# Four 32-column groups of TensorE for the sample group's attention and scans of a hybrid decoder step

## The chip, the cores and the metric

One Trainium2 chip, one of its cores. The time is that of one launch on the device in microseconds, and the median of several runs counts. TensorE (PE) multiplies matrices into PSUM, VectorE (DVE), ScalarE (ACT) and GpSimd (POOL) work on vectors, and the queues of SyncE (SP) and of POOL issue most DMAs. All values are float32. `F32R` (fp32r) is the type that a matmul takes in one pass; plain `F32` operands go in full precision. Where the kernel wants more precision than F32R has, it splits an operand into a rounded part "hi" and a remainder "lo" and adds the products.

## The reference

One layer of a decoder for two groups of tokens with the same weights: a prompt (256 tokens) and a sample group (8 batches of 4 tokens, 32 in all). Each token has 2048 channels. For both groups:

```python
xn = rmsnorm(x);  z, xbc, dt, q, k, v, r, g, gate_a, gate_b = split(xn @ w_in)
a = ssd_scan(silu(conv(xbc)), dt, state_ssd) ; a = rmsnorm(a * silu(z)) @ w_ssd_out      # 32 heads in 4 groups
b = gla_scan(q, k, v, log_sigmoid(g @ w_gla_gate), state_gla) ; b = ... * silu(r) @ w_gla_out  # 4 heads
h = x + (sigmoid(gate_a) * a + sigmoid(gate_b) * b) @ w_mix_out
h = h + softmax(q K^T) V @ w_co        # q = rmsnorm(h) @ w_cq; 4 heads of 512, 256 memory rows per batch
h = h + (silu(gt) * up) @ w_down       # causal ConvFFN of width 5632
y = rmsnorm(h)
```

Every batch of the sample group has its own recurrent states (SSD: 32 x 64 x 128, GLA: 4 x 256 x 512) and its own memory keys and values (256 x 4 x 512 each). The prompt starts from zero states, and its memory keys and values come from `mem_prompt @ w_ck` and `@ w_cv`, which are outputs too. The new states are outputs as well.

## The kernel before

Activations lie transposed: 128 channels on the partitions, the 288 tokens (256 of the prompt, 32 of the sample group) along the free dimension. A projection (`proj_w`, line 112) keeps 128 weight columns in the array and streams the 288 tokens. Weights come as `raw` tiles of up to 512 KB through a ring of three (SP's queue); `wsplit` (lines 92 to 98) makes hi on ScalarE and lo on VectorE; per 128 x 128 block there are three matmuls, hi by hi (line 127), hi by lo (128) and lo by hi (131). One `yield` of it, a step, is 12 matmuls. The first stage (memory keys and values, `mem_proj`, lines 306 to 310) streams 512 weight columns instead. `run(proj_w(dt_load, 48, ...))` between its parts makes dt (32 columns) and the input of the GLA gate (16 columns).

The scans and the attention are generators. `weave(main, bg, n_main, n_bg)` interleaves the steps of a projection (main) with those of a scan (bg), so that the next unit's projection covers the present unit's scan. There are eight units, SSD groups 0 to 3 and GLA heads 0 to 3, with the planned numbers of steps in `N_MAIN` and `N_BG`. After that the program is ordered by Tile's scheduler, by program order and readiness, with an order for each engine that is fixed at build time.

The parts that matter here, all for the 32 sample tokens. They differ by batch, so each batch needs its own right-hand operand, and its 4 tokens are put into a block of 64 weight columns that is zero elsewhere (`diag2`, line 170: 32 columns hi, 32 columns lo):

- SSD (`ssd_scan`, line 620): the state of each batch is transposed (line 777) and split; `inter` (760 to 763) multiplies the 64 columns with its hi and its lo, 512 wide, all adding into one PSUM tile of 64 rows. Line 753 is the product within a batch, head by head. Lines 722 to 724 are the prompt's own heads, in pairs that write to rows 0 to 63 and 64 to 127. Line 812 folds hi and lo rows together by a matmul with `fold` (64 rows).
- GLA (`gla_scan`, line 921): each batch and key half is split and multiplied likewise (`inter`, 1024 and 1025; line 1027 adds the product within the batch); line 1040 makes the state update, line 1053 folds. Lines 951 and 954 make the masks' products, line 874 the gate, with 16 rows. State tiles come from a ring of four, `c4`, that input states (`sin`), output states (`so`) and others share.
- Attention: for each head, `sample_scores` (line 1238) transposes the 8 batches' keys (line 1213), splits them and adds the scores (1254, 1255), 256 wide; `attend` folds them (1268), makes the softmax, transposes it (1287), splits the values and multiplies (1311, 1312), 512 wide, and folds four times (1329). `sample_scores` isn't woven with anything; `attend` is woven with the query projection of the next head, and that of the last head with nothing.
- `h` (the residual stream) sits in SBUF in the one buffer `bigf` from line 1141 on, loaded from a copy of x in DRAM by four DMAs.

Of the kernel before, what the change touches and what calls it, by code (L numbers as in the profile page):

```python
# [36 lines left out]
N_BG = [48] * 4 + [52] * 4  # L37
# [3 lines left out]
def hybrid_step(ctx: ExitStack, tc: tile.TileContext, I: dict, O: list):  # L41
# [32 lines left out]
    fold = const.tile([2 * NS, NS], F32, name="fold")  # L74
    V.tensor_tensor(fold, ident[0:2 * NS, 0:NS], ident[0:2 * NS, NS:2 * NS], ALU.add)
# [36 lines left out]
    def proj_w(load, ncol, X, nk, cons, N=T):  # L112
# [3 lines left out]
        for k0 in range(0, nk, 4):  # L116
            kn = min(4, nk - k0)
            raw = load(k0, kn)
            for s0 in range(0, kn, 2):
# [14 lines left out]
                if k0 + s0 == 2:  # L134
                    flush()
# [34 lines left out]
    def diag2(blk, src):  # L170

        f = blk.rearrange("p b t -> p (b t)")
        w = 2 * NS + NL
        hi = bass.AP(f.tensor, f.offset, [list(f.ap[0]), [w, NB], [1, NL]])
        lo = bass.AP(f.tensor, f.offset + NS, [list(f.ap[0]), [w, NB], [1, NL]])
        split(hi, lo, src.rearrange("p (b l) -> p b l", l=NL))
# [21 lines left out]
    def rstd_from(pl, ssq, n, four=False):  # L198
# [11 lines left out]
    smask = p1.tile([NS, NS], F32, name="smask")  # L210
    G.affine_select(smask, causal[0:NS, 0:NS], pattern=[[-4, NB], [0, NL]], compare_op=ALU.is_ge, fill=0.0, base=0,
                    channel_multiplier=1)
    smaski = p1.tile([NS, NS], I32, name="smaski")
    V.tensor_copy(smaski, smask)
# [5 lines left out]
    rm_s = p1.tile([P, T], F32, name="rm_s")  # L220
    rm_g = p1.tile([P, T], F32, name="rm_g")
    for rm, c in ((rm_s, 128), (rm_g, 64)):
# [3 lines left out]
    acumT = p1.tile([32, T], F32, name="acumT")  # L226
    lrT = p1.tile([48, T], F32, name="lrT")
    tokc = p1.tile([P, 3, 64], F32, name="tokc")
    wtok = p1.tile([P, 4, 32], F32, name="wtok")
    eas = p1.tile([2 * NS, 32], F32, name="eas")  # L230
# [3 lines left out]
    cblk = p1.tile([P, NB, 2 * NS], F32R, name="cblk")  # L234
    att = p1.tile([P, 2, P], F32, name="att")
    ats = p1.tile([NS, NS], F32, name="ats")
    qblk = p1.tile([P, 2, NB, 2 * NS], F32R, name="qblk")
    G.memset(cblk.bitcast(F32), 0.0)
    G.memset(att, 0.0)
    G.memset(ats, 0.0)  # L240
    G.memset(qblk.bitcast(F32), 0.0)
# [3 lines left out]
    x_d = dram.tile([P, KT, T], F32, name="x_d")  # L245

    X = halves(bigr, "xn")
    with pool("p0") as p0:
# [5 lines left out]
        bsel_rep = bsel_rep.rearrange("p r t -> p (r t)")  # L254
        gm_f = p0.tile([P, P], F32, name="gm_f")
# [61 lines left out]
        def prep_mem(kk):  # L317
# [5 lines left out]
            if kk % 2:  # L323
                sq = p0.tile([P, D], F32, name="junk")
                i, q = kk // 2 % 2, kk // 4
                S.activation(sq[:, 0:512], mt[:, i, q * 512:(q + 1) * 512], ACT.Square, accum_out=mss[:, i, q:q + 1])
# [36 lines left out]
        def x_norm():  # L363
            ss = p0.tile([P, 3], F32, name="ss")
# [32 lines left out]
        def x_prep():  # L397
# [23 lines left out]
            V.tensor_copy(bmask, a[:, 0:NB])  # L421

        weave(mem_proj(I["w_cv"], 0, o_pmv), x_norm(), KT, 12)
# [4 lines left out]
        dte = p0.tile([32, T], F32, name="dte")  # L428
        dtT = p0.tile([32, T], F32, name="dtT")
        acol = p0.tile([32, 1], F32, name="acol")  # L430

        def dt_load(k0, kn):
            raw = wp.tile([P, kn, 48], F32, tag="raw", bufs=RB, name="raw")
            for o, c0, n in ((0, O_DT, 32), (32, O_G, 16)):
                nc.sync.dma_start(out=raw[:, :, o:o + n],
                                  in_=I["w_in"][k0 * P:(k0 + kn) * P, c0:c0 + n].rearrange("(k p) n -> p k n", p=P))
            return raw

        def dt_cons(j, a):
            S.activation(dtx, a[0:32], ACT.Identity, bias=dtb)  # L440
            S.copy(lrT[32:48, :], a[32:48])

        run(proj_w(dt_load, 48, X, KT, dt_cons))

        def dt_prep():
# [7 lines left out]
            V.tensor_tensor_scan(acumT, rm_s[0:32, :], dte, 0.0, ALU.mult, ALU.add)  # L453
# [31 lines left out]
            V.tensor_copy(tokc.rearrange("p c x -> p (c x)"), a[:, 0:192])  # L485
            yield
# [8 lines left out]
            S.activation(eas, tokc[0:2 * NS, 2, 32:64], ACT.Exp)  # L495
# [18 lines left out]
    def b2(name):  # L514
        return pa.tile([P, 512], F32, tag="b2", bufs=9, name=name)

    def r2(name):
        return pa.tile([P, 512], F32R, tag="r2", bufs=6, name=name)

    def c4(shape, name):  # L520
        return pa.tile(shape, F32, tag="c4", bufs=4, name=name)
# [7 lines left out]
    def conv_cache(n, ch0, cache):  # L529

        a = mm_tile()
        TR(a[0:27 * n, 0:P], cache.rearrange("p c t -> p (c t)"), ident)
        st = b2("cst")[0:27 * n, 0:P]
        S.copy(st, a[0:27 * n, 0:P])
        nc.sync.dma_start(out=o_pconv[0, :, ch0:ch0 + n * P].rearrange("k (t p) -> k t p", p=P), in_=st[0:3 * n])
        nc.sync.dma_start(out=o_sconv.rearrange("b k c -> (b k) c")[:, ch0:ch0 + n * P].rearrange("k (t p) -> k t p", p=P),
                          in_=st[3 * n:27 * n])
# [49 lines left out]
    def ssd_proj(g, out):  # L587
        xsT = a4("xsT")
        cache = pa.tile([P, 27, 4], F32, tag="cache", bufs=2, name="cache")
        for j2 in range(2):  # L590
            def cons(j, a, j2=j2):
                t = j2 * 2 + j
                conv_silu(4 * g + t, a, xsT[:, t, :], cache[:, :, t])
            yield from proj(I["w_in"], O_XBC + 512 * g + 256 * j2, 256, X, KT, cons)
        late.append(lambda cache=cache: conv_cache(4, 512 * g, cache))
        if g % 2 == 0:
            bcp = [e2("bc") for _ in range(2)]
            for w in range(2):
# [949 lines left out]
```

## Time and profile before

| | us |
|---|---|
| runs, median (lowest to highest of 3) | 2676.44 (2671.35 to 2677.17) |
| the profiled execution, its own time | 2672.26 |
| its span, first to last instruction | 2670.5 |
| TensorE busy | 2648.0 (99%) |
| VectorE busy | 1824.6 (68%) |
| ScalarE busy | 1467.0 (55%) |
| GpSimd busy | 276.0 (10%) |
| DMA | 509.11 MB, mean 191 GB/s |

The stages by the profile: memory keys and values to 208 us (last record of line 310), the eight units' scans to 1237 us (line 833), the second gate to 1375 us (line 1135), the mixing projection to 1488 us (line 1168), the attention with its first query projection to 1716 us (line 1329), the rest of the output projection and the ConvFFN to the end. The page lists engine shares, the chain of waits that ended last (from the last instruction back to whatever released each step), groups of instructions and DMA issues. The timeline lists instructions in order of time: start, length, engine, line, operation, result<-operands, partitions x elements, count. A matmul's length includes its way through the array, and neighbours overlap; so the distance between two starts tells what a matmul costs the engine. A plain F32 matmul shows as two records.

### The profile page before, as it was taken

The numbers are of one execution on the slowest core, as the hardware profiler recorded it, in microseconds if no ns is written. First come the engines' busy times: TensorE is split into PE (matmuls) and PEld (weight loads), VectorE is DVE, ScalarE is ACT, GpSimd is POOL, SyncE is SP. The second block draws the span as 40 slices with busy tenths as digits, with TensorE's granted clock in tenths as the row PEclk, the third lists the DMA queues.
The fourth block names the chain that finished last, engine by engine and source line by source line (L and its number), as shares of the span: only waits on it lengthen the run. The fifth ranks groups of instructions, "written<-read, shape, count | busy, mean of one in ns | idle before, by whom it ended". The sixth has DMA issues, their size and how long they took to land.

```text
span 2670.5 us, 50978 instructions
## 1 busy us (share of the span) xinstructions
PE 2648.0 (99%) x19191; PEld 2537.7 (95%) x19191; DVE 1824.6 (68%) x3809; ACT 1467.0 (55%) x2958; POOL 276.0 (10%) x360
## 2 busy tenths in 40 slices
PE   9999999999999999999999999999999999999998
PEld 7889999999999999999999999899999999999998
DVE  5656777786676667666656676666777677676765
ACT  7656566564646564645445565555545455454545
POOL 2001101000000000000010122202202021110200
PEclk9999999999999999999999999999999999999999
DMA  8676666655575757677665677555555555555553
GB/s 257 204 223 190 177 189 190 188 175 176 169 249 183 230 174 236 196 238 221 185 224 176 205 232 250 185 167 161 171 170 167 167 160 175 169 166 167 164 171 130
DMA packets 433170, 509.11 MB, mean 191 GB/s; under 512 B 22504, under 2 KB 383896, under 8 KB 432604
## 3 DMA queue, kind: packets, MB, share of 16 engines
q1 hardware_dynamic: 408684, 423.16, 51.4%
q0 software_dynamic: 24208, 82.70, 9.5%
q8 instruction: 150, 2.46, 0.4%
q14 instruction: 96, 0.79, 0.1%
q10 hardware_dynamic: 32, 0.01, 0.0%
HBM read 462.65 MB, written 43.12 MB: 189 GB/s over the span
## 4 chain that ended last, share of the span: by engine, by line
PE 96%; DMA 1%; DVE 1%; ACT 1%; issue 0%; SPq 0%; DVEq 0%; ACTq 0%; POOLq 0%
PE acc L127 26%; PE acc L128 26%; PE acc L131 26%; PE acc L306 2%; PE acc L310 2%; PE acc L307 2%; PE acc L1213 1%; PE la L1255 1%; PE mm L1213 1%; PE la L1254 1%; PE mm L1040 1%; PE la L1024 1%; PE la L1025 1%; PE mm L777 1%; DMA raw<-in_w_mix_out_dram 1%; PE mm L998 1%
## 5 line engine op out<-in xcount | busy, mean ns | idle before, releaser
L95 ACT CAST whi<-raw 128x512 fp32r<-128x512 f32 (+1 forms) x1464 | 897.0, 618 | 1011.3 <-PE acc L128 821.1
L97 DVE TENSOR_TENSOR wlo<-raw,whi 128x512 fp32r<-128x512 f32 (+1 forms) x1464 | 987.3, 686 | 677.7 <-ACT whi L95 656.6
L127 PE MATMUL acc<-xn,whi 128*128 128x288 f32 (+1 forms) x1936 | 550.1, 299 | 0.0
L128 PE MATMUL acc<-xn,whi 128*128 128x288 f32 (+1 forms) x1936 | 541.2, 295 | 0.0
L131 PE MATMUL acc<-xn,wlo 128*128 128x288 f32 (+1 forms) x1936 | 411.7, 294 | 0.0
L127 PE MATMUL acc<-hf,whi 128*128 128x288 f32 x1408 | 396.2, 296 | 0.0
L128 PE MATMUL acc<-hf,whi 128*128 128x288 f32 x1408 | 393.6, 295 | 0.0
L127 PEld LDWEIGHTS acc<-xn,whi 128*128 128x128 f32 (+1 forms) x1936 | 362.7, 187 | 13.3 <-issue 4.6
L128 PEld LDWEIGHTS acc<-xn,whi 128*128 128x128 f32 (+1 forms) x1936 | 363.1, 188 | 6.6 <-issue 2.6
L131 PEld LDWEIGHTS acc<-xn,wlo 128*128 128x128 f32 (+1 forms) x1936 | 309.8, 187 | 0.5 <-DVE wlo L97 0.2
L131 PE MATMUL acc<-hf,wlo 128*128 128x288 f32 x1408 | 302.2, 296 | 0.0
L128 PEld LDWEIGHTS acc<-hf,whi 128*128 128x128 f32 x1408 | 265.2, 188 | 0.1
L127 PEld LDWEIGHTS acc<-hf,whi 128*128 128x128 f32 x1408 | 264.7, 188 | 0.1
L131 PEld LDWEIGHTS acc<-hf,wlo 128*128 128x128 f32 x1408 | 225.4, 188 | 0.0
L128 PE MATMUL acc<-pr,whi 128*128 128x288 f32 x704 | 196.5, 295 | 0.0
L127 PE MATMUL acc<-pr,whi 128*128 128x288 f32 x704 | 195.7, 294 | 0.0
L127 PE MATMUL acc<-un,whi 128*128 128x288 f32 x512 | 151.8, 312 | 1.2 <-ACT ma L849 1.0
L131 PE MATMUL acc<-pr,wlo 128*128 128x288 f32 x704 | 147.7, 290 | 0.0
L128 PE MATMUL acc<-un,whi 128*128 128x288 f32 x512 | 143.7, 295 | 0.0
L1380 POOL COPY fsp<-fst 128x16 f32<-128x16 f32 x88 | 104.7, 1214 | 337.1 <-ACT fcg L1386 96.5
L128 PEld LDWEIGHTS acc<-pr,whi 128*128 128x128 f32 x704 | 132.3, 188 | 0.0
L127 PEld LDWEIGHTS acc<-pr,whi 128*128 128x128 f32 x704 | 132.1, 188 | 0.0
(521 smaller groups left out, 4676.3 us busy)
## 6 DMA issues: line engine op xcount, KB each, us to landing
raw<-in_w_in_dram SPq DMA_DIRECT2D x240, 512.0 KB
raw<-in_w_up_dram SPq DMA_DIRECT2D x176, 512.0 KB
raw<-in_w_down_dram SPq DMA_DIRECT2D x88, 512.0 KB
raw<-in_w_ck_dram SPq DMA_DIRECT2D x32, 512.0 KB
raw<-in_w_cv_dram SPq DMA_DIRECT2D x32, 512.0 KB
raw<-in_w_ssd_out_dram SPq DMA_DIRECT2D x32, 512.0 KB
sin<-in_state_gla_dram POOLq DMA_DIRECT2D x32, 512.0 KB, 4.8
out_dram<-so SPq DMA_DIRECT2D x32, 512.0 KB
```

The costliest lines, as they stand in the source:

```text
L95: S.copy(hi, raw)
L97: V.tensor_tensor(lo, raw, hi, ALU.subtract)
L127: MM(a, hi[:, k, cs], xh, start=(k0 + s0 + k == 0), stop=False)
L128: MM(a, hi[:, k, cs], xl, start=False, stop=False)
L131: MM(a, lo[:, k, cs], xh, start=False, stop=(k0 + s0 + k == nk - 1))
L306: MM(accs[m], mn_hi[:, kk, ms_], hi[:, 0, :], start=(kk == 0), stop=False)
L307: MM(accs[m], mn_lo[:, kk, ms_], hi[:, 0, :], start=False, stop=False)
L310: MM(accs[m], mn_hi[:, kk, ms_], lo[:, 0, :], start=False, stop=(kk == KT - 1))
L777: TR(a[:, t * P:(t + 1) * P], sin[:, e, t * P:(t + 1) * P], ident)
L998: MM(a, kt[:, i, k * P:(k + 1) * P], vt[i], start=True, stop=True)
L1213: TR(a[:, d * 256 + m * P:d * 256 + (m + 1) * P], kv[:, m, dd * P:(dd + 1) * P], ident)
L1380: G.tensor_copy(sp[:, :, 0:2], st.rearrange("p (b k) -> p b k", k=2))
```

## The change

For the sample tokens the split operands go. Each batch takes one plain F32 matmul whose 32 weight columns go to one of four groups of 32 output rows, `32 j` to `32 j + 31`; batch `4 q + j` takes group j, and the four groups are added up at the end by one matmul with `fold4` (128 rows). The matmuls of several batches stand together in one run: SSD 8 and two for the product within the batch, GLA 8 twice, scores 16 twice, values 16 once, per group or head. The states are updated in place (`so` goes, `c4` has 6 buffers). Products with fewer than 128 rows or columns are widened to 128 by copies or by zeros (masks, gate, softmax transposes, folds). The prompt's SSD heads go four at a time. `h` is written to DRAM during the mixing projection and read back before the output projection, since the first four batches' values take its buffer; x comes in 8 smaller loads. The last head is woven with the first steps of the output projection. The diff, cut to its core:

```diff
-N_BG = [48] * 4 + [52] * 4
+N_BG = [48] * 4 + [38] * 4
...
-                if k0 + s0 == 2:
+                if k0 + s0 == min(4, nk - 2):
                     flush()
...
+    def diag(blk, src):
+        f = blk.rearrange("p b t -> p (b t)")
+        V.tensor_copy(bass.AP(f.tensor, f.offset, [list(f.ap[0]), [NS + NL, NB], [1, NL]]),
+                      src.rearrange("p (b l) -> p b l", l=NL))
...
             for i in (2, 0, 1):
-                junk = p0.tile([P, D], F32, name="junk")
-                S.activation(junk, xts[i], ACT.Square, accum_out=ss[:, i:i + 1])
-                yield
-                yield
+                for q in range(4):
+                    junk = p0.tile([P, 512], F32, name="junk")
+                    S.activation(junk, xts[i][:, q * 512:(q + 1) * 512], ACT.Square, accum_out=sp4[:, i, q:q + 1])
+                    yield
...
         def dt_load(k0, kn):
-            raw = wp.tile([P, kn, 48], F32, tag="raw", bufs=RB, name="raw")
+            raw = wp.tile([P, kn, 112], F32, tag="raw", bufs=RB, name="raw")
...
+            for k in range(kn):
+                G.tensor_copy(raw[:, k, 48:112].rearrange("p (r n) -> p r n", n=16),
+                              raw[:, k, 32:48].unsqueeze(1).to_broadcast([P, 4, 16]))
             return raw
...
-        run(proj_w(dt_load, 48, X, KT, dt_cons))
+        run(proj_w(dt_load, 112, X, KT, dt_cons))
...
+        mab = pa.tile([P, 2, NS], F32, tag="mab", bufs=1, name="mab")
+        for r in range(4):
+            G.dma_start(out=mab[r * NS:(r + 1) * NS], in_=acum_d[h0:h0 + 8, SEQ:T].rearrange("(a r) t -> r a t", r=4)[r].partition_broadcast(NS))
...
-            MM(a[0:n, t0:t0 + n], bT[:, t0:t0 + n], cT[:, t0:t0 + n], start=True, stop=True)
+            MM(a[:, t0:t0 + n], bT[:, t0:t0 + n] if i < 2 else bsr[:, 0, :], cT[:, t0:t0 + n], start=True, stop=True)
...
+                for w in range(2):
+                    o = w * SEQ
+                    for s in range(3):
+                        for e in range(2):
...
+                            if s == 0:
+                                MM(a[rows, o:o + P], xdt[0][:, hs], pm[:, q, 0:P], start=True, stop=True)
+                            elif s == 1:
+                                MM(a[rows, o + P:o + SEQ], xdt[1][:, hs], pm[:, q, P:SEQ], start=True, stop=False)
+                            else:
+                                MM(a[rows, o + P:o + SEQ], st0[:, hs], pea[:, q, :], start=False, stop=True)
...
         def inter():
-            b, sh, sl = pend.pop(0)
-            MM(ysi[0:2 * NS, :], cblk[:, b, :], sh, start=(b == 0), stop=False)
-            MM(ysi[0:2 * NS, :], cblk[:, b, :], sl, start=False, stop=(b == NB - 1))
+            ysi.append(la_tile())
+            ysa.append(mm_tile())
+            for q in (1, 0):
+                for j in (3, 2, 1, 0):
+                    MM(ysi[0][NS * j:NS * j + NS, :], cdm[:, 4 * q + j, :], sts[4 * q + j], start=(q == 1), stop=(q == 0))
+            for r in range(2):
+                MM(ysa[0][NS * r:NS * r + NS, 256 * r:256 * r + 256], mss[:, r, :], xds[:, 256 * r:256 * r + 256],
+                   start=True, stop=True)
...
             for t2 in range(2):
+                if q == 3 and t2 == 1:
+                    inter()
+                    yield
...
-                MM(a[:, 0:T], gw[:, k * P:(k + 1) * P], lrT[32:48, :], start=True, stop=True)
+                MM(a[:, 0:T], gw3[:, k * P:(k + 1) * P], lr3, start=True, stop=True)
...
-                MM(a[0:64, 288 + 64 * i:352 + 64 * i], kd[:, k, P * i:P * i + 64], qe[:, k, P * i + 64:P * i + P],
+                MM(a[:, 288 + 64 * i:352 + 64 * i], kd[:, k, P * i:P * i + P], qe[:, k, P * i + 64:P * i + P],
...
+        MM(osa, atsl, vst, start=True, stop=False)
+        for q in range(2):
+            for k in (1, 0):
+                for j in (3, 2, 1, 0):
+                    b = 4 * q + j
+                    MM(osa[NS * j:NS * j + NS, :], qdm[:, k, b, :], sins[b][:, k, :], start=False, stop=(q == 1 and k == 0))
+            yield
+            for b in range(4 * q, 4 * q + 4):
...
+                for k in range(2):
+                    a = mm_tile()
+                    MM(a, kb[:, k * P:(k + 1) * P], vst, start=True, stop=True)
+                    V.scalar_tensor_tensor(sin[:, k, :], sin[:, k, :], eb[:, k, SEQ + 4 * b + 3:SEQ + 4 * b + 4], a,
+                                           ALU.mult, ALU.add)
+                    yield
+                nc.sync.dma_start(out=o_sgla[b, h].rearrange("(k p) v -> p k v", p=P), in_=sin)
+                if b + 4 < NB:
+                    load_state(b + 4)
...
+        run(proj(I["w_mix_out"], 256 * j2, 256, mx, KT, cons))
+        G.dma_start(out=h_d[:, 2 * j2:2 * j2 + 2, :], in_=hx[j2])
+        if j2 + 3 < KT // 2:
+            load_x(j2 + 3)
...
+        vq = big.tile([P, 4, 2, 512], F32, tag="bigf", bufs=1, name="vq")
...
+        def scores(q):
+            for d in range(4):
+                for j in (3, 2, 1, 0):
+                    b = 4 * q + j
+                    MM(ssc[NS * j:NS * j + NS, 0:256], xq[:, d, b, :], kT[b][:, d, :], start=(q == 0 and d == 0),
+                       stop=(q == 1 and d == 3))
...
+        for q in (1, 0):
+            for m in range(2):
+                for j in (3, 2, 1, 0):
+                    MM(osa[NS * j:NS * j + NS, :], pms[:, m, 4 * q + j, :], vcs[4 * q + j][:, m, :],
+                       start=(q == 1 and m == 0), stop=(q == 0 and m == 1))
...
+        a = mm_tile()
+        for d in range(4):
+            MM(a[:, d * NS:(d + 1) * NS], os_[:, d * P:(d + 1) * P], fold4, start=True, stop=True)
...
     for hd in range(4):
-        ssc = la_tile()
-        sample_scores(hd, ssc)
-        kp, vp = mem_rows(o_pmk[0, :, hd, :], "kp"), mem_rows(o_pmv[0, :, hd, :], "vp")
-        if hd < 3:
-            weave(q_proj(hd + 1), attend(hd, ssc, kp, vp), 16, 20)
-        else:
-            run(attend(hd, ssc, kp, vp))
+        main = q_proj(hd + 1) if hd < 3 else chain(steps(wo[0], 6), steps(wo[1], 6))
+        weave(main, attend(hd), 16 if hd < 3 else 12, 21)
...
+    for j2 in range(KT // 2):
+        G.dma_start(out=h[:, 2 * j2:2 * j2 + 2, :], in_=h_d[:, 2 * j2:2 * j2 + 2, :])
```

More of the change, by code (lines that the diff above doesn't have):

```diff
@@ L976, in gla_scan @@
         stack_r(vst, a)
-        vts = b2("vts")
-        S.copy(vts[0:NS], a[0:NS, :])
         yield
@@ L1014, in gla_scan @@
         nc.sync.dma_start(out=o_pgla[0, h].rearrange("(k p) v -> p k v", p=P), in_=sprev)
-        load_state(0)
-        load_state(1)
+        for b in range(4):
+            load_state(b)
         yield
         osa = la_tile()
-        pend = []
-        def inter():
-            b, k, sh, sl = pend.pop(0)
-            MM(osa[0:2 * NS, :], qblk[:, k, b, :], sh, start=(b == 0 and k == 0), stop=False)
-            MM(osa[0:2 * NS, :], qblk[:, k, b, :], sl, start=False, stop=(b == NB - 1 and k == 1))
-            if b == 0 and k == 0:
-                MM(osa[0:NS, :], ats, vts[0:NS, :], start=False, stop=False)
@@ L1048, in gla_scan @@
         os_ = b2("os")
[L1049 removed]
+        S.copy(os_, osa)
         yield
@@ L1259, in attend, with rows @@
-    def attend(hd, ssc, kp, vp):
-        ss2 = px.tile([2 * NS, 256], F32, tag="ss2", bufs=1, name="ss2")
-        S.copy(ss2, ssc[0:2 * NS, 0:256])
+    def attend(hd):
+        xq = xqm[hd % 2]
+        loads = [(I["cache_mem_k"][b, :, hd, :], "kc") for b in range(NB)]
+        loads += [(o_pmk[0, :, hd, :], "kp"), (o_pmv[0, :, hd, :], "vp")]
+        loads += [(I["cache_mem_v"][b, :, hd, :], "vc") for b in range(4, NB)]
+        got = []
+        vq = big.tile([P, 4, 2, 512], F32, tag="bigf", bufs=1, name="vq")
+        def rows():
+            while loads and len(got) < 4:
+                got.append(mem_rows(*loads.pop(0)))
+            return got.pop(0)
+        ssc = la_tile()
+        kT = []
+        def scores(q):
[4 more added lines that the diff above has]
+                       stop=(q == 1 and d == 3))
+        for b in range(NB):
+            kc = rows()
+            kT.append(k4("kT"))
+            for d2 in range(2):
+                a = transpose_half(kc, d2)
+                (S.copy if d2 else V.tensor_copy)(kT[b][:, 2 * d2:2 * d2 + 2, :], a)
+            if b < 4:
+                G.dma_start(out=vq[:, b], in_=I["cache_mem_v"][b, :, hd, :].rearrange("(m p) d -> p m d", p=P))
+            yield
+            if b == 4:
+                scores(0)
+                yield
+        kp = rows()
@@ L1266, in attend @@
         yield
[L1267 to L1270 removed]
+        scores(1)
         yield
@@ L1284, in attend @@
             yield
+        vp = rows()
+        vh, vl = v2("vph"), v2("vpl")
+        split(vh, vl, vp)
         a = mm_tile()
         for m in range(2):
-            TR(a[:, m * NS:(m + 1) * NS], pr[:, m * P:(m + 1) * P], ident[0:NS, 0:NS])
+            TR(a[:, m * P:(m + 1) * P], pr[:, m * P:(m + 1) * P], ident)
         for m in range(2):
-            diag2(ptb[:, m], a[:, m * NS:(m + 1) * NS])
-        vcs = [mem_rows(I["cache_mem_v"][b, :, hd, :], "vc") for b in range(2)]
+            f, g = pms[:, m].rearrange("p b t -> p (b t)"), a[:, m * P:(m + 1) * P]
+            V.tensor_copy(bass.AP(f.tensor, f.offset, [list(f.ap[0]), [4 * (NS + NL), 2], [NS + NL, 4], [1, NL]]),
+                          bass.AP(g.tensor, g.offset, [list(g.ap[0]), [4 * NL, 2], [NS + NL, 4], [1, NL]]))
         yield
@@ L1358, in hybrid_step @@
     hf = halves(bigr, "hf")
-    run(residual(I["w_co"], co, vec("norm_ffn"), hf))
+    h = bigf("h")
+    for j2 in range(KT // 2):
+        G.dma_start(out=h[:, 2 * j2:2 * j2 + 2, :], in_=h_d[:, 2 * j2:2 * j2 + 2, :])
+    acc = pb.tile([P, T], F32, tag="sqa", bufs=1, name="sqa")
+    res.update(h=h, hf=hf, acc=acc)
+    run(*wo)
+    rst.append(acc)
     rf = []
```

388 lines of the change are left out of this document (182 added, 206 removed).

## The prediction

> **What bounds the kernel now.** I read the page first: engine shares, then the chain of waits.
>
> ```profile
> PE 2648.0 (99%) x19191; PEld 2537.7 (95%) x19191; DVE 1824.6 (68%) x3809; ACT 1467.0 (55%) x2958; POOL 276.0 (10%) x360
> ...
> PE 96%; DMA 1%; DVE 1%; ACT 1%; issue 0%; SPq 0%; DVEq 0%; ACTq 0%; POOLq 0%
> ```
>
> TensorE is busy throughout and is 96% of the chain that ended last. So the time changes by the TensorE time that the edit takes out, less what it puts in, less new stalls; the ScalarE and VectorE splits that disappear are off the path. A matmul's mean length in a group is no price, since neighbours overlap. I price by the distance between starts in the timeline of TensorE (first number: start in us, second: length). Four prices follow.
>
> Plain fp32, 512 columns (L998), between projection matmuls:
>
> ```profile
> 728.21 1.02 PE L998 MATMUL mm<-vt,kt 128*128 128x512 f32 x2
> 728.66 0.69 PE L127 MATMUL acc<-xn,whi 128*128 128x288 f32 x1
> 729.20 0.29 PE L128 MATMUL acc<-xn,whi 128*128 128x288 f32 x1
> ```
>
> One matmul leaves two records. A projection matmul takes 0.13 (rows below), so L127 really began at 729.20 - 0.13 = 729.07, and L998 took 0.86: 0.43 a record of 512 columns, in proportion for fewer.
>
> The split form (hi and lo in fp32r), which the sample stages use now:
>
> ```profile
> 746.56 0.40 PE L1024 MATMUL la<-sh,qblk 128*64 128x512 f32 x1
> 746.79 0.40 PE L1025 MATMUL la<-sl,qblk 128*64 128x512 f32 x1
> 747.03 0.37 PE L127 MATMUL acc<-un,whi 128*128 128x288 f32 x1
> ```
>
> 0.235 each. For the scores, one batch of the key loop:
>
> ```profile
> 1510.69 0.60 PE L1213 MATMUL mm<-ident,kc 128*128 128x128 f32 x4
> 1511.13 0.60 PE L1213 MATMUL acc<-ident,kc 128*128 128x128 f32 x4
> ...
> 1512.49 0.27 PE L1213 MATMUL mm<-ident,kc 128*128 128x128 f32 x1
> ```
>
> A transpose is 0.11 (0.44 for four; the price of any record with 128 weight columns and few moving ones). The batch takes 1.80; less 8 transposes, 0.92 is left for 8 score matmuls of 256 columns: 0.115 each.
>
> The gap around a narrow run, that is, one using fewer than 128 rows, or fp32 with fewer than 128 output columns:
>
> ```profile
> 750.03 0.43 PE L131 MATMUL acc<-un,wlo 128*128 128x288 f32 x2
> 750.40 1.04 PE L1027 MATMUL la<-vts,ats 32*32 32x512 f32 x2
> ...
> 751.61 0.29 PE L128 MATMUL acc<-un,whi 128*128 128x288 f32 x1
> ```
>
> L131 is done at 750.03 + 0.26 = 750.29, projection is back at 751.61 - 0.13 = 751.48: 1.19 for two records of 0.43. The gap is 0.33 a run, however long the run.
>
> Last, whether groups of columns work at the same time. Before has this in L722 to L724 (two 64-column halves):
>
> ```profile
> 301.92 0.43 PE L131 MATMUL acc<-xn,wlo 128*128 128x288 f32 x2
> 302.28 0.43 PE L722 MATMUL mm<-m,xdt 128*64 128x128 f32 x2
> 302.55 0.27 PE L723 MATMUL mm<-m,xdt 128*64 128x128 f32 x1
> 302.56 0.32 PE L722 MATMUL mm<-m,xdt 128*64 128x128 f32 x1
> 302.66 0.27 PE L723 MATMUL mm<-m,xdt 128*64 128x128 f32 x1
> ...
> 303.59 0.30 PE L128 MATMUL acc<-xn,whi 128*128 128x288 f32 x1
> ```
>
> The second half's L722 (302.56) runs beside the first half's L723 (302.55, 302.66, full pace of 0.11), and starts ahead of its second record. 12 records take 303.46 - 302.18 = 1.28 with the gap; one after another they would be 1.3 without it. Two groups are shown at full speed, four are not.
>
> **The change, stage by stage.** Each batch now takes one plain fp32 matmul with 32 output columns instead of two split ones; four batches fill the four column groups. If all four work together, a round of four costs one matmul: 0.86 at 512 columns, 0.43 at 256.
>
> Attention, per head. Scores: 8 x 4 x 2 x 0.115 = 7.4, now 8 rounds x 0.43 = 3.4 in two runs (0.66). Values: 8 x 2 x 2 x 0.235 = 7.5, now 4 x 0.86 = 3.4 in one run (0.33). The fold of the scores (L1268: 0.43 and a gap) goes; the 32-row transposes (L1287) become two full ones (+0.1, a gap less); four folds of the output (L1329) become one:
>
> ```profile
> 1554.32 0.28 PE L1328 MATMUL mm<-pTh,vpl 128*128 128x256 f32 x1
> 1554.53 0.41 PE L1329 MATMUL mm<-fold,os 64*128 64x32 f32 x2
> ...
> 1555.10 0.30 PE L128 MATMUL acc<-hn,whi 128*128 128x288 f32 x1
> ```
>
> Each is 554.97 - 554.44 = 0.53 (last digits), four 2.1; the new one, 128 rows, no gap, 8 records: 0.9. Per head 3.3 + 3.7 + 0.76 + 0.2 + 1.2 = 9.2; four heads **37**.
>
> GLA, per head:
>
> ```profile
> 1065.85 1.16 PE mm L874 x4
> ...
> 1103.44 1.13 PE mm L951 x12
> 1104.57 0.61 PE mm L954 x8
> ```
>
> (chain of waits: start, time on the chain.) State products: 32 x 0.235 = 7.5, now 3.4 in two runs (0.66): 3.4. The gate (L874), 1.16 + 0.2 of its gap, becomes two fp32r matmuls, 0.26: 1.1. L1027's 1.19 becomes one of 0.235: 0.95. The fold loses its gap: 0.33. L951 and L954, 1.74 and the rest of a gap, about 1.9, widen to 20 records of 0.11 = 2.2: -0.3. Sum 5.5, four heads **22**.
>
> SSD, per group. State products: 16 x 0.235 = 3.8, now 2 x 0.86 + 0.33 = 2.05: 1.7. The intra product (L753, 16 records of 64 columns, 0.9, and a gap) becomes two concurrent matmuls in the same run, 0.43: 0.8. L722 to L724: four runs of 1.28 become two of 12 x 0.11 + 0.33 = 1.65: 1.8. L645 and L812 lose a gap each, about 0.5 together. Sum 4.8, four groups **19**.
>
> Sum: 78 us less TensorE work.
>
> The Trainium skill, "TensorE: Matmul & The Clock Gate", section "Measured speedup vs the span model", gives 2.38x for three column tiles of 512. That is 79% of ideal; as an estimate from that page, the 48 us of grouped rounds here would become about 61 and the saving 13 us less. The rows above show no such loss for two groups.
>
> What is put in. *Projection of dt.* 64 copied columns make each of its loads wait for four POOL copies, with the wsplits and matmuls of L127 queued behind them and the weight ring (three buffers) held.
>
> ```profile
> L1380 POOL COPY fsp<-fst 128x16 f32<-128x16 f32 x88 | 104.7, 1214 | 337.1 <-ACT fcg L1386 96.5 <-DVE fst L1372 69.1 <-ACT fca L1386 56.1
> L547 POOL COPY sp<-scst 128x24 f32<-128x24 f32 x24 | 11.7, 503 | 53.6 <-DVE bc L555 31.7 <-DVE xsT L555 20.1 <-ACT whi L95 1.8
> ...
> 104.91 3.35 SPq L435 DMA_DIRECT2D raw<-in_w_in_dram  x4
> ...
> 117.77 0.43 PE L131 MATMUL acc<-xn,wlo 128*48 128x288 f32 x2
> ```
>
> The last loads are issued at 107 to 108, the stage ends at 118. At 0.5 us a copy a load needs 2 us, hidden by that distance; at 1.2 the 16 copies need 19 from about 102, and the stage ends some 6 late. I take 2.
>
> *The runs' operands.* A run cannot begin until four batches' data are there; what waits behind it on TensorE is the projection. The tightest is GLA's second run: loads of batches 6 and 7 need buffers whose stores have landed.
>
> ```profile
> sin<-in_state_gla_dram POOLq DMA_DIRECT2D x32, 512.0 KB, 4.8
> ```
>
> A load takes 4.8, a store taken as the same: 9.6 from the end of batch 1 to the data of batch 7. Between lie 4 steps of the scan, each with 64/38 = 1.7 projection steps (12 matmuls of 0.13, 1.6) and one 0.235: 4 x 2.9 = 11.7. Just covered. If not, the run is cut up: single groups at 0.86 instead of a round, 8 x 0.86 - 1.7 and three more gaps = 6.2 a head. Between 0 and 25 for four heads; I take 5.
>
> *h in DRAM.* x in 8 loads instead of 4, 8 stores, 8 loads back, all issued by POOL (10% busy). Behind the reload, which waits for the last value run, stand FFN loads that are not due for tens of us. Bandwidth: attention saves 9 of 58 us a head for the same bytes.
>
> ```profile
> 1379.00:1395.00 16.00, 14.08 (x107) 13.84 (x106) 4.41 (x8) 3.36 (x7) 5.38 (x7) 1.00 1.04 399
> 1556.00:1614.00 58.00, 58.00 (x427) 53.21 (x426) 41.21 (x75) 34.54 (x66) 12.79 (x18) 1.00 0.72 238
> ```
>
> 238 GB/s become 238 x 58/49 = 282, under the 399 seen at 1379 (last column): nothing. The last head beside w_co is nearly nothing either: its idle time is small, and the new fold at its end has nothing left beside it (+2).
>
> *Stalls that may go.*
>
> ```profile
> 35.64 0.58 PE L306 MATMUL acc<-whi,mn_hi 128*128 128x512 f32 x1 [3.00 <-ACT whi L95]
> ...
> 1379.77 14.18 DMA raw<-in_w_mix_out_dram
> ...
> 1707.30 0.45 PE L1311 MATMUL la<-vh,ptb 128*64 128x512 f32 x1 [0.69 <-ACT vh L167]
> ```
>
> The first is ScalarE in long squares of x, which are cut in four; the second a weight load beside the burst that loads h, which is spread out; the third a value split. Together 0 to 6, I take 4.
>
> Net: 78 - 2 - 5 - 2 + 4 = 73. The profiled execution took 2672.3 (span 2670.5): 2599. The median of the runs, 2676.4, lies 4.2 higher: **2603**.
>
> **Rivals.**
>
> *Two at a time* (0.08). Each matmul is two records, and a group's second needs its first. If starts were in strict program order, group 2 could begin only when group 3's second record begins, and so on: a round would take twice as long. The rounds are 4 x (3.4 + 3.4 + 3.4 + 1.7) = 48, so +48: 2651, still faster. Against it: 302.56 starts between 302.55 and 302.66, the two records of one instruction. The strict order is what the Trainium skill states in "TensorE: Matmul & The Clock Gate", section "The mechanism" (matmuls first in, first out); by those rows it does not hold between column groups.
>
> *Runs that are not long, or groups that lose pace* (0.22). The order on TensorE follows readiness; 1510.69 and the score matmuls before it already mix. If each of the 32 new runs (3 a head in attention, 2 in GLA, 3 a group in SSD) falls into three, 64 gaps cost 21; GLA's bound alone is 25. Time 2612 to 2640.
>
> *Slower: groups in turn* (0.03). If 32-column fp32 matmuls don't overlap, the 48 us of rounds are 192: 2603 + 144 = 2747. It turns slower when fewer than 192/(48 + 73) = 1.6 groups work on average. Against it: two do now.
>
> *The saving is eaten by waits in several stages* (0.04): 2655 to 2680.
>
> **How the numbers follow.** The forecast has 0.63: four groups, runs mostly whole, 2590 to 2612 (all put-in costs at zero and stalls at 6 give 84 less, 2592). The range reaches over most of the second rival, 2590 to 2640; 2 in 10 are left for two at a time and beyond, and below. Faster by over 0.2% (5.4 us, about what a measurement of this kernel can tell): the first three cases and a quarter of the last, 0.94; same 0.03; slower 0.03.
>
> **What would show it.** Right: in the timeline four groups' records start within 0.1 us of each other, a run of 8 matmuls of 512 lasts about 2.05 with its gap; attention about 49 us a head; GLA units 5 to 6 us shorter. Wrong: a run of 8 lasting 3.8 (two at a time) or 7; the 32 runs showing as 100; TensorE idle at 110 to 125 behind POOL copies, or before GLA's second run behind a load.

## The result, and the profile after

The changed kernel takes 2608.04 us (median of 4 runs, 2604.51 to 2609.79), the kernel before beside it 2675.92 (2671.35 to 2677.17): ratio 0.9748, 95% interval [0.9731, 0.9765]. Two more measurements of the same pair are told below as controls: 0.9732 [0.9709, 0.9754] and 0.9745 [0.9732, 0.9758]. The forecast was 2603, from 2590 to 2640. The profiled execution of after took 2607.92, so 64 us less than the one of before, where the forecast had 73.

The page of after, its span and engine shares:

```profile
span 2606.2 us, 50491 instructions
...
PE 2576.2 (99%) x19123; PEld 2473.3 (95%) x19123; DVE 1718.2 (66%) x3683; ACT 1376.2 (53%) x2796; POOL 308.2 (12%) x425
```

TensorE is 72 us less busy (2648.0 before), and it is still what bounds the kernel; ScalarE and VectorE lost 91 and 106 us, most of it splits, and these were off the path. The span fell by 64.3: TensorE now also stands still for 7.5 us more.

The new runs, in the timeline of TensorE (start, length of the group of records, then the operation). First a value run, then a GLA run:

```profile
1510.66 0.42 PE L133 MATMUL acc<-hn,wlo 128*128 128x288 f32 x2
1511.01 1.92 PE L1380 MATMUL la<-vc,pms 128*32 128x512 f32 x16
1512.76 1.90 PE L1380 MATMUL la<-vq,pms 128*32 128x512 f32 x16
1514.59 0.39 PE L1387 MATMUL mm<-pTh,vph 128*128 128x256 f32 x1
1514.81 0.28 PE L1388 MATMUL mm<-pTl,vph 128*128 128x256 f32 x1
```

```profile
780.23 0.41 PE L133 MATMUL acc<-xn,wlo 128*128 128x288 f32 x2
780.57 1.92 PE L1078 MATMUL la<-sin,qdm 128*32 128x512 f32 x16
782.43 0.40 PE L129 MATMUL acc<-xn,whi 128*128 128x288 f32 x1
782.66 0.29 PE L130 MATMUL acc<-xn,whi 128*128 128x288 f32 x1
```

Read as in the prediction: the projection is done at 780.23 + 0.26 = 780.49 and back at 782.66 - 0.13 = 782.53. The GLA run takes 2.04, forecast 2.05. The value run starts with the end of L133 at 1510.92 and hands over at 1514.81 - 0.115 = 1514.695 (L1387 streams 256 columns, 0.115): 3.78 for eight rounds of 0.43 and a gap of 0.34, forecast 3.77. Four groups do work at full pace together. The Trainium skill, "TensorE: Matmul & The Clock Gate", section "Measured speedup vs the span model", has three column tiles at 2.38 times one; no such loss shows here with four.

For where the rest went I took, from the timeline, the length of each stage less its projection matmuls (0.131 each, 0.228 with 512 columns), that is, the TensorE time of all else, idle time included. An SSD or GLA unit ends at the matmul of its norm (L833 before, L879 after). In us:

| stage | before | after, three profiles | forecast | e4 | e5 | e6 |
|---|---|---|---|---|---|---|
| memory projections, dt | 26.7 | 27.0, 26.7, 26.5 | | 24.2 | 29.3 | 28.4 |
| SSD group 0 with its projection | 23.7 | 26.4, 24.5, 27.4 | | 19.3 | 25.8 | 19.7 |
| SSD group 1 | 25.4 | 24.2, 26.4, 25.3 | | 26.2 | 20.5 | 20.0 |
| SSD group 2 | 23.7 | 18.9, 19.0, 19.3 | | 19.3 | 19.2 | 19.3 |
| SSD group 3 | 26.1 | 20.9, 20.6, 20.8 | | 20.9 | 20.7 | 20.7 |
| SSD, sum | 98.9 | 90.4, 90.5, 92.8 | 79.9 | 85.7 | 86.2 | 79.7 |
| GLA, four heads | 109.2 | 91.2, 89.3, 90.7 | 92 | 89.9 | 90.1 | 90.9 |
| second gate, mix | 4.5 | 2.3, 2.3, 2.3 | | 2.3 | 2.7 | 2.7 |
| attention, output projection | 134.0 | 98.1, 98.2, 97.3 | 98 | 98.0 | 98.4 | 98.0 |
| FFN, end | 28.1 | 28.2, 28.2, 28.2 | 28 | 28.2 | 28.2 | 28.2 |
| sum | 401.4 | 337.2, 335.2, 337.8 | 328 | 328.3 | 334.9 | 327.9 |

(e4 to e6 are experiments, below.) Attention and GLA are at their forecast. SSD is 11 to 13 us short of it, all in its first two groups. What TensorE waits for there, in the list of waits of after (us in total, times, longest):

```profile
PE acc L313 <- ACT whi L97: 5.2, 2, 3.4
PE acc L129 <- ACT whi L97: 2.8, 1, 2.8
PE la L807 <- ACT st L824: 2.0, 1, 2.0
PE mm L834 <- ACT st L824: 1.7, 1, 1.7
PE acc L133 <- DVE wlo L99: 1.4, 1, 1.4
```

L313 is the wait at the start, which was there before. The other four lie at 249, 345, 445 and 447 us, in groups 0 and 1, and are new. The first, in the timeline of TensorE:

```profile
249.10 0.43 PE L133 MATMUL acc<-xn,wlo 128*128 128x288 f32 x2
252.34 0.61 PE L129 MATMUL acc<-xn,whi 128*128 128x288 f32 x1 [2.80 <-ACT whi L97]
252.74 0.44 PE L130 MATMUL acc<-xn,whi 128*128 128x288 f32 x1
...
257.78 0.68 PE L133 MATMUL acc<-xn,wlo 128*128 128x288 f32 x2
258.26 0.37 PE L129 MATMUL acc<-xn,whi 128*128 128x288 f32 x1
258.47 0.29 PE L130 MATMUL acc<-xn,whi 128*128 128x288 f32 x1
```

After the wait the starts are 0.24 apart until 258.26 and 0.13 after it: 24 matmuls at half the clock (the granted clock, the share of its full clock that the profile shows for TensorE, is 0.50 there), 2.7 us on top of the 2.8. The Trainium skill, "TensorE: Matmul & The Clock Gate", section "What's actually happening", has the clock fall to half after at least one idle window of about 3.4 us; here it came after 2.8 to 3.1 us (249.36 to 252.5). The length of the wait alone does not decide it in these runs. At the same place the clock was kept after 2.2 us in one more profile of the changed kernel (c1) and halved after 2.1 us in the other (c2); in two of the experiments below it was kept after 2.8 us (e3) and halved after 1.9 us (e7), as the granted clock shows (the third value from the right; the first row is e3, the second e7):

```profile
249.00:252.00 3.00, 2.15 (x15) 1.99 (x16) 2.17 (x6) 2.83 (x10) 0.00 (x0) 1.00 0.32 113
249.00:252.00 3.00, 2.07 (x9) 2.07 (x10) 2.09 (x6) 2.73 (x8) 0.00 (x0) 0.67 0.68 242
```

The same happens in group 1, around 445 us: there the clock is halved for 6.8 us in c1 and for 3.4 us in c2, and not in the profile of after. A stretch of 6.8 us at half the clock costs 3.4 us; that is most of why the rows of groups 0 and 1 differ from profile to profile.

### The profile page after: what moved, and what is told of

Its sections match the earlier page's. It is cut to its first block, busy times and chain, and to the rows that moved or that the text cites. A ratio compares the mean times of both kernels' runs of the same rounds, so it can differ in the third digit from the quotient of the medians.

```text
span 2606.2 us, 50491 instructions
## 1 busy us (share of the span) xinstructions
PE 2576.2 (99%) x19123; PEld 2473.3 (95%) x19123; DVE 1718.2 (66%) x3683; ACT 1376.2 (53%) x2796; POOL 308.2 (12%) x425
## 5 line engine op out<-in xcount | busy, mean ns | idle before, releaser
L133 PE MATMUL acc<-xn,wlo 128*128 128x288 f32 (+1 forms) x1936 | 413.0, 295 | 1.4 <-DVE wlo L99 1.4
L133 PEld LDWEIGHTS acc<-xn,wlo 128*128 128x128 f32 (+1 forms) x1936 | 311.3, 188 | 1.8 <-DVE wlo L99 1.7
L133 PE MATMUL acc<-hf,wlo 128*128 128x288 f32 x1408 | 302.2, 296 | 0.0
L133 PEld LDWEIGHTS acc<-hf,wlo 128*128 128x128 f32 x1408 | 225.4, 188 | 0.0
L133 PE MATMUL acc<-pr,wlo 128*128 128x288 f32 x704 | 147.8, 291 | 0.0
```

The costliest lines, as they stand in the source:

```text
L133: MM(a, lo[:, k, cs], xh, start=False, stop=(k0 + s0 + k == nk - 1))
```

## Where the late weights come from

ScalarE's cast that this wait is for, before and after (idle time of ScalarE ahead of it in brackets), and GpSimd's issues in after:

```profile
246.86 1.14 ACT L95 CAST whi<-raw 128x512 fp32r<-128x512 f32 x2 [4.83 <-DMA raw<-in_w_in_dram]
```

```profile
251.66 1.14 ACT L97 CAST whi<-raw 128x512 fp32r<-128x512 f32 x2 [9.64 <-DMA raw<-in_w_in_dram]
```

```profile
240.37 3.71 POOL L672 DMA_DIRECT2D sin<-in_state_ssd_dram  x5
```

The weight load lands 4.8 us later than before. Beside it run five state loads of 256 KB each, which before were not issued until 303 us. Three theories: A, these loads slow the weight load (the tag that their tiles share has six buffers instead of four, the masks of the prompt's heads take two of them instead of four, and in group 0 nothing makes the loads wait); B, the flush that was moved one step later puts cache stores ahead of the weight load on SyncE; C, the raw weight ring of three buffers is too short now that TensorE is faster.

**c1, the control.** 

> The changed kernel once more, on the same chip as the three runs beside it, so that they are compared with it and not with a run of another day. Expected 2608 us, within 2 us, and a ratio to the kernel before of 0.975.

Measured: 2605.62 (2604.71 to 2607.7), ratio 0.9732.

**e1, two state tiles held.**

```diff
             sin = c4([P, 2, 512], "sin")
+            if g == 0 and q >= 2:
+                G.tensor_copy(sin[:, :, 0:1], sts[2 * q - 4][:, 0:2].unsqueeze(2))
```

(A condition in the output projection, not shown, is changed too and has no effect: the same 32 copies run as in the changed kernel.)

> Only the loads of the third and fourth state tile of SSD group 0 are held back (a two-element copy on GpSimd into each tile, from a state that the scan has already turned, goes ahead of its load), so that in the 240s the state queue carries what it carried before the change. It is meant for the new stall at 249 us, where the split weights come 2.8 us late and TensorE then runs at half its clock for about 7 us, together some 5 us. Theory A, the early state loads slow the weight load: the stall and the half clock go, 2603 us. Rival B, the flush that was moved one step later puts the cache stores ahead of the weight load on SyncE: no change here, 2608. Rival C, the weights are late for want of buffers, whatever is beside them: no change here and none with the flush moved back, 2608 for both.

Measured: 2605.37 (2603.32 to 2607.72). The wait stayed, 2.9 us. This looked like the end of theory A, but the trace showed the test to be too weak: the first two tiles, 1 MB, still went out at 238.6 us.

**e2, the flush back.**

```diff
-                if k0 + s0 == min(4, nk - 2):
+                if k0 + s0 == 2:
```

> Only the flush of the cache stores goes back to the step at which the kernel before had it. Rival B (see the run with two states held): the weight load of 240.8 us is issued 1.6 us earlier, as before, the wait of 2.8 us at 249 us falls to about 1.2, too short for the half clock, and the time to about 2603. Theories A and C: no change at 249 us, 2608 within 2.

Measured: 2607.13 (2605.07 to 2609.16). The wait changed its shape (0.4 for the hi part at 252.5, 3.0 for the lo part at 256.3) and is no shorter in sum, and the half clock is there again. Theory B falls.

**e4, all four state tiles held.**

```diff
             sin = c4([P, 2, 512], "sin")
+            if g == 0:
+                G.tensor_copy(sin[:, :, 0:1], (st0 if q < 2 else sts[2 * q - 4])[:, 0:2].unsqueeze(2))
```

> All four state tiles of SSD group 0 are held back, the first two too (with two held, 1 MB of state still went out at 238.6 us, and the kernel before sends none of it before 303). In the run with two held the wait at 249 us stayed. Theory A, state loads beside the weight loads: now the wait and the half clock go, 3 to 5 us, about 2601. Rival C, buffers or order of the loads, whatever is beside them: the wait stays, 2605.

Measured: 2601.97 (2599.27 to 2603.02), ratio 0.9719 [0.9704, 0.9734]. The cast waits for the landing as long as in the kernel before:

```profile
244.06 1.14 ACT L97 CAST whi<-raw 128x512 fp32r<-128x512 f32 x2 [4.85 <-DMA raw<-in_w_in_dram]
```

The wait of TensorE for this cast and the half clock behind it are gone (0.85 us of a wait for a lo part is left at 251), and group 0, between 24.5 and 27.4 in the changed kernel, falls to 19.3. From its issue to this cast the weight load takes 6.1 us here and 10.8 in after. Theory A is shown for group 0, by the trace; the times alone would not show it, since the interval overlaps those of the controls. Group 1, with 26.2, did not get shorter; 3.4 of it is a half clock of 6.8 us from 437 us on.

**e5, a fourth raw weight buffer** up to the end of GLA (the small tiles that make room for it are left out here).

```diff
+        turn.append(0)
+        if more and len(turn) % 4 == 0:
+            raw = more[0].tile([P, src.shape[1], src.shape[2]], F32, tag="rawx", bufs=1, name="raw")
+        else:
+            raw = wp.tile([P, src.shape[1], src.shape[2]], F32, tag="raw", bufs=RB, name="raw")
```

> A fourth buffer for raw weights up to the end of the GLA stage (every fourth load goes to a tile of its own; room for it by letting some small tiles of the SSD and the GLA stage share their places). Theory C, TensorE is now ahead of the weight loads in the SSD stage, and that is where the forecast 19 us there became 13: the late weights at 249, 345 and 446 us go, each 1.5 to 3, and with them the half clock; 6 to 9 us less than the change, 2597 to 2600. Rival, the casts of ScalarE stand in their queue behind other work and not behind the weight's landing: no change, 2605.

Measured: 2605.35 (2605.11 to 2606.45): no gain in the time, and yet half of theory C holds. The lines of its list of waits with the longest ones:

```profile
PE acc L319 <- ACT whi L97: 5.0, 3, 2.5
PE acc L139 <- DVE wlo L99: 3.2, 2, 3.0
...
PE acc L135 <- ACT whi L97: 1.2, 1, 1.2
```

The waits for st (L807, L834) are gone, and group 1 falls from about 25 to 20.5. In group 0 the wait only moves: 3.0 us at 257, with the half clock behind it. The first stage is longer by 2.5 in this profile; its ring of buffers is the old one, and the cause stays open (this stage lies between 24 and 29 us in all profiles but that of e10, which changes it).

**e6, both.** 

> The fourth raw weight buffer and all four state tiles of SSD group 0 held back, together. Where both theories are right, for different stalls: 2595. Where only one of them is, the time of that one alone.

Measured: 2600.43 (2598.65 to 2602.2), ratio 0.9715 [0.97, 0.973]. Both groups are at about 20, SSD is 19.2 less than before, and the forecast of this term was 19. No half clock is left between the start and the end of this profile. So the term was right as a price of the work, and what was missing were two kinds of late weights, with the half clock that came behind them: in group 0 state loads beside the weight load, in group 1 a ring without slack. As a whole e6 is not told apart from e4 by the medians (1.5 us); the trace tells them apart.

## What the long runs rest on

**e3, group by group.** The loop over the four groups is made the outer one in all long runs; as an example the value run:

```diff
-        for q in (1, 0):
-            for m in range(2):
-                for j in (3, 2, 1, 0):
+        for j in (3, 2, 1, 0):
+            for q in (1, 0):
+                for m in range(2):
```

> In the attention runs, the GLA runs and the SSD inter run, the loop over the four column groups is made the outer one: all matmuls of one group, then all of the next. The same matmuls on the same groups, only in another order. Theory: matmuls begin in program order, and one that needs its own group's predecessor holds all behind it; so only the last of one group and the first of the next overlap. The values run then takes about 16 x 0.86 - 3 x 0.43 + 0.33 = 12.8 us in place of 3.8, a scores run 6.6 in place of 2.06, a GLA run 5.9 in place of 2.05, the SSD run about 3.9 more; in all 4 x (9 + 9) + 8 x 3.9 + 4 x 3.9 = 119 more, 2727 us. Rival: each group works through its own queue, the order does not matter, 2608.

Measured: 2648.53 (one run), 41 to 43 more: neither. A value run:

```profile
1514.37 0.43 PE L133 MATMUL acc<-hn,wlo 128*128 128x288 f32 x2
1514.73 1.90 PE L1380 MATMUL la<-vc,pms 128*32 128x512 f32 x4
1516.47 0.59 PE L1380 MATMUL la<-vq,pms 128*32 128x512 f32 x1
1516.47 0.62 PE L1380 MATMUL la<-vc,pms 128*32 128x512 f32 x1
...
1521.71 1.88 PE L1380 MATMUL la<-vq,pms 128*32 128x512 f32 x4
1523.52 0.39 PE L1387 MATMUL mm<-pTh,vph 128*128 128x256 f32 x1
```

Each group has 8 records here, four with vc and then four with vq. The first group runs its four vc records alone (1514.73 to 1516.47, 4 x 0.43); then its vq records run beside the next group's vc records, pair by pair, 12 pairs until 1521.71; the last four are alone again. 20 steps of 0.43 are 8.6; it takes 8.9. The next group thus begins while three records of the group ahead of it still wait behind the running one, and not before. A score run, 32 records of 0.215, takes 4.7 with its gap, again 20 steps. In a GLA run each group has only four records, and there the order costs nothing:

```profile
779.58 1.95 PE L1078 MATMUL la<-sin,qdm 128*32 128x512 f32 x16 [0.16 <-DMA sin<-in_state_gla_dram]
781.46 0.40 PE L129 MATMUL acc<-xn,whi 128*128 128x288 f32 x1
```

All of the loss is in attention: its row of the table is 139.8 here, 42 more; by these run lengths it would be 4 heads x (2 x 2.6 + 5.2) = 42. The order within a run matters here with eight records of a group in a row and not with four, and with eight it leaves two groups at work: the time of the prediction's first rival, 2651, by another mechanism. The Trainium skill, "TensorE: Matmul & The Clock Gate", section "The mechanism", says that matmuls start and end strictly in program order. Between column groups this trace speaks against it: the second group's first record starts at 1516.47, ahead of three records of the first group that stand before it in the program. (The order in the program is that of the loops in the source; the order fixed at build time is not in the trace.) The kernel before shows the same with two groups, in the prediction's rows of L722 to L724: the second half's first record (302.56) starts with the third of the first half's six (302.55), while three still wait. The 12 records take eight steps so, not six, which is where its 1.28 comes from; the prediction read these rows as two groups at full speed.

**e7, runs cut up.** After each round of four groups in the score, value and GLA runs a step of the projection may come between; as an example:

```diff
                     MM(osa[NS * j:NS * j + NS, :], pms[:, m, 4 * q + j, :], vcs[4 * q + j][:, m, :],
                        start=(q == 1 and m == 0), stop=(q == 0 and m == 1))
-        yield
+                yield
```

(The number of steps that the weave spreads over the projection is raised to match, from 38 to 40 in GLA and from 21 to 30 in attention.)

> Each score, value and GLA run is cut at every round of four groups, with projection work between the pieces, as far as the order on TensorE then keeps them apart: in its program 46 pieces in place of 22. Nothing else changes. Theory: each narrow run costs a gap of 0.33 us, however long: 24 more gaps, 8 us, 2613. Rival: the gap is not the run's but an entry's share of its operands' waits, and is hidden beside other work: 2605.

Measured: 2618.33 (2615.38 to 2620.93), ratio 0.9781 [0.9765, 0.9797], 10 to 13 above the changed kernel. One piece of a GLA run:

```profile
781.39 0.43 PE L133 MATMUL acc<-xn,wlo 128*128 128x288 f32 x2
781.75 1.06 PE L1078 MATMUL la<-sin,qdm 128*32 128x512 f32 x8
782.74 0.40 PE L129 MATMUL acc<-xn,whi 128*128 128x288 f32 x1
782.98 0.30 PE L130 MATMUL acc<-xn,whi 128*128 128x288 f32 x1
```

From 781.65 to 782.85: 1.20 for two records of 0.43, so the gap is 0.34 for a piece of 8 records, as for a run of 16 (0.32 above) or 32 (0.34). The trace has the expected 46 pieces. 18 more of them in attention cost 7.2 there, 6 more in GLA 3 to 5, of which 1.0 is a new wait for a state load. The gap is the price of a piece; the "long" in long runs is worth about what the expectation said, 8, and a little more.

**c2, a second control.** 

> The changed kernel again, beside the three of this call: 2606 us within 2.

Measured: 2607.34 (2604.5 to 2610.15), ratio 0.9745.

**e8, the last head alone.**

```diff
-        main = q_proj(hd + 1) if hd < 3 else chain(steps(wo[0], 6), steps(wo[1], 6))
-        weave(main, attend(hd), 16 if hd < 3 else 12, 21)
+        if hd < 3:
+            weave(q_proj(hd + 1), attend(hd), 16, 21)
+        else:
+            run(attend(hd))
```

> The last head of the attention runs alone, and the output projection starts after it, as in the kernel before; all else as changed. The prediction put this part at nothing, since the last head's idle time is small. By that theory 2606, within 2 of the changed kernel. Rival: with nothing beside it the last head waits at every score, softmax and transpose step; an attention head spends about 6 us of its own matmuls between these steps, and if each of some 8 steps waits 1 us, 2614.

Measured: 2611.34 (2609.3 to 2613.95), ratio 0.976 [0.9747, 0.9774], 4.0 more; the attention row is 101.0 against 97.3 to 98.2. The times alone are hardly apart, their ranges overlap; the row is. The last head of e8:

```profile
1624.67 1.93 PE L1317 MATMUL la<-kT,xqm 128*32 128x256 f32 x32
1627.63 1.06 PE L1268 MATMUL mm<-ident,kc 128*128 128x128 f32 x8 [1.02 <-DMA kc<-in_cache_mem_k_dram]
...
1632.35 1.93 PE L1317 MATMUL la<-kT,xqm 128*32 128x256 f32 x32
...
1637.18 0.38 PE L1361 MATMUL mm<-ident,prs 128*128 128x128 f32 x2
1637.32 0.38 PE L130 MATMUL acc<-co,whi 128*128 128x288 f32 x1
...
1638.26 0.30 PE L1370 MATMUL mm<-ident,prp 128*128 128x128 f32 x1
...
1639.42 1.92 PE L1380 MATMUL la<-vc,pms 128*32 128x512 f32 x16
1641.28 0.55 PE L1370 MATMUL mm<-ident,prp 128*128 128x128 f32 x3
1641.76 1.92 PE L1380 MATMUL la<-vq,pms 128*32 128x512 f32 x16
```

What TensorE waits for are the loads of the cached keys. The stretch from the first score run to the second, one run and 32 transposes, would take 2.05 + 32 x 0.11 = 5.6 without a wait and takes 7.7; in it (1625 to 1634) the DMA engines are busy throughout at 384 GB/s. In c2 projection steps stand between the same transposes, and no such wait is in its list. Between softmax, transposes and value run TensorE does not wait even in e8: matmuls of the output projection (operand co) fill the stretch, since the scheduler moves them there. The value run falls into two pieces, one more gap. So neither the rival's 8 us nor its waits at each step came; the weave is worth about 3, 2.1 of it this wait.

**e9, h in SBUF.** h takes the place of vq again, the values of all batches go through the five row buffers, in two runs:

```diff
-        vq = big.tile([P, 4, 2, 512], F32, tag="bigf", bufs=1, name="vq")
...
-        vcs = [vq[:, b] for b in range(4)] + [rows() for _ in range(4)]
         for q in (1, 0):
+            vcs = [rows() for _ in range(4)]
...
-        G.dma_start(out=h_d[:, 2 * j2:2 * j2 + 2, :], in_=hx[j2])
```

> h stays in SBUF during the attention: x is loaded into it in eight loads once the second gate has freed the place, there is no store and no reload, and the cached values go through the five row buffers, so that the value run becomes two runs of 16 records, the second when its loads are there. Theory: four more gaps at 0.3 to 0.5 each, and the weight wait of about 2 us at 1380 us is back (the loads of x come in one burst again): 3 to 4 us more, 2609 to 2610. Rival: the second value run waits for its four loads, about 5 us each head: 2626.

Measured: 2622.14 (2615.84 to 2626.58), ratio 0.9799 [0.9783, 0.9815], 15 more. The first line of its list of waits within attention:

```profile
PE la L1375 <- DMA vc<-in_cache_mem_v_dram: 10.4, 4, 3.0
```

The second value run of each head waits up to 3.0 us for its loads: 10.4 in four heads, where the rival had about 20. The attention row is 109.7, 12 more (a half clock of 3.4 us in the second head is in it); second gate and mix 4.1, the weight wait beside the burst that loads x is back.

**e10, the version that the runs pointed to:** e6, and the statistics and the scaling of the first memory projection moved behind the first casts of the next.

```diff
+            if prep is not None:
+                late.append(evac)
+            else:
+                evac()
...
+                if kk == 6:
+                    flush()
```

> The version to which the runs so far point: all four state tiles of SSD group 0 held back, the fourth raw weight buffer, and the two table loads of ScalarE with the scaling of the first memory projection moved behind the first weight casts of the next (they stand between the two, where TensorE waits 2.0 to 3.4 us at 33 us). Theory: the sum of the three, 2600.4 less 2 to 3: 2598, 8 below the changed kernel. Rival: the wait at 33 us only moves to the next landing of weights: 2600.

Measured: 2603.54 (2602.3 to 2604.22), ratio 0.973 [0.9717, 0.9744]. SSD stays at its 80, but the first stage rises to 31.9:

```profile
PE acc L321 <- ACT whi L97: 6.4, 4, 2.1
```

There are four waits in place of two or three. The first long one (2.1 us) ends with a cast that waits for its weight to land, as the rival said:

```profile
40.85 0.62 ACT L97 CAST whi<-raw 128x512 fp32r<-128x512 f32 x1 [6.44 <-DMA raw<-in_w_cv_dram]
```

Behind it the table loads and the scaling now stand between casts that TensorE needs (0.8 and 2.1 us). The wait at the start is not cheaper elsewhere; e6 without this edit is the fastest version that ran.

## Why the prediction was right, and where it was not

- **Four groups at full pace, prices of the records and of the gap:** right. GLA run 2.04 for 2.05, value run 3.78 for 3.77, gap 0.32 to 0.34 for 0.33. "Two at a time" and "groups in turn" did not come. e3 shows that the time of the first of them is what the other order of the loop would have given, though not by strict order.
- **Attention, 37 less, 2 given back, 0.7 of a value split:** 35.7 forecast, 35.8 to 36.7 measured. That the last head beside the output projection is worth "nearly nothing" failed: it is worth about 3 (e8), since without projection steps between them the new head's transposes wait for the loads of the keys. The sum hides it, because the change brought both at once. "h in DRAM: nothing" is right for its cost; but the single value run rests on it, and by e9 attention would be 12 worse without it, 10.4 of it waits for loads.
- **GLA, 22 less and 5 given back:** 18 to 20 less. Two first runs fell into two pieces (0.7), and the profiles of the changed kernel show no wait for a state load (of the experiments e3 has one of 0.16 and e7 one of 1.0); the bound of 25 was far off.
- **SSD, 19 less:** this is the term that was mis-sized, with 6 to 8.5 measured. The work did fall by 19 (e6). The step that failed is "the runs' operands": it looked for waits at the new runs, above all in GLA, where none came, and not at the projection weights of the SSD stage, whose waits came instead (one of 2.0 us, L807, stands at the SSD run itself). The rows for it were there: the change gives the state tiles six buffers, so in group 0 nothing holds their loads back, and the weight ring already left ScalarE waiting 4.8 us at 246.86 in the kernel before. Of a buffer count that is raised, the transfers that now start earlier must be priced too.
- **Projection of dt, 2:** 0. The copies take 0.3 us each, not 0.5 to 1.2:

```profile
L454 POOL COPY raw<-raw 128x64 f32<-128x64 f32 x16 | 3.8, 284 | 18.0 <-DVE xn L166 13.1 <-DMA raw<-in_w_in_dram 3.9 <-issue 1.1
```

  TensorE is busy without a break there, as the windows of after show (length, busy time of TensorE first):

```profile
104.00:112.00 8.00, 8.00 (x41) 6.32 (x40) 4.13 (x13) 2.58 (x6) 3.02 (x15) 1.00 0.38 74
112.00:120.00 8.00, 8.00 (x57) 7.70 (x56) 3.05 (x7) 3.86 (x9) 1.15 (x3) 1.00 0.71 234
```

- **Stalls that go, 4:** the weight wait in the mix went (2.2) and the value split; the wait at the start did not: 2.1 to 3.4 for 3.0 before. Cutting the squares did not touch it, since two table loads of 1.3 us stand in the same place, as they did before.

In sum: 73 forecast, 64 measured in the profiled executions, and 73.5 in e6, where the waits in SSD are gone. By the medians of the runs it is 68 for the changed kernel (71 and 68 in the controls) and 76 for e6, since the profiled execution of before is 4 us faster than its median; so the miss is 2 to 5 us in the time that was forecast, and 9 in the profiles. That it is no larger is partly luck: SSD was short by 11 to 13 and the wait at the start stayed, while GLA and the copies of dt came out better by 3 to 5. That e6 meets the forecast so closely is partly luck too, since its first stage was 1.7 longer and the copies of dt cost nothing.

## What to carry to other kernels

When TensorE gets faster, look at the transfers beside it next: a stage whose weights just arrived in time will now wait, and a buffer count raised for one stage starts loads earlier in another. Matmuls on the four column groups need to go round the groups; four records of one group in a row cost nothing here, eight made a run 2.4 times as long. A piece of narrow work cost a third of a microsecond at each length that ran, 2 to 32 records, so long runs are worth something, and the memory that lets their operands be there in time is worth more: with the residual tensor kept out of DRAM, attention was 12 us longer, nearly all of it waits for values.

## What was not expected of the hardware

- The run through column groups goes on past three waiting records of one group, and not past a fourth: with the group loop outermost, value and score runs take 20 steps in place of 8, and GLA runs with four records a group are unharmed.
- Five state loads of 256 KB, issued by GpSimd at 240 us, made a weight load of 512 KB on the other queue land 4.8 us later.
- The half clock after a wait of 2.8 us cost as much again, 2.7 us; waits of 1.9 to 2.8 us brought it in some profiles and not in others.
